# Second block: factors copied from PSUM, two products behind 1/rms, wide sums

## The chip, the cores and the metric

One Trainium2 chip, one of its eight cores. The metric is the time of one execution on the device in microseconds (us), here the median of three runs. The engines are named as in the profile: PE is TensorE's matmuls, PEld its weight loads, DVE is VectorE, ACT is ScalarE, POOL is GpSimd, SP issues DMAs.

## What is computed

Two transformer blocks run one after the other on x, 512 tokens by 1024 channels in float32. The change lies in the second block, whose two layers have this form:

```python
def second_block(x, ...):
    for i in range(DEPTH):                      # 2
        hn = rms_norm(x, norm_gains[i, 0])
        if kind == 0:
            m = stick_breaking_attention(hn, ...)
        elif kind == 1:
            m = dilated_attention(hn, ...)
        x = x + rms_norm(m, norm_gains[i, 1])
        f = conv_ffn(rms_norm(x, norm_gains[i, 2]), ...)
        x = x + rms_norm(f, norm_gains[i, 3])
    return x
```

with `rms_norm(x, g) = x * rsqrt(mean(x*x) + EPS) * g` over the 1024 channels of a token. So four times a matrix product m or f (the output projection of an attention, or the down projection of the feed-forward) is normalized, multiplied by a gain and added to x; after the first three of them the next layer's first projection follows.

## The kernel before

x lies in SBUF with channels on partitions: 8 chunks of 128 channels by 512 tokens. Every projection splits both operands into a high part (`hi`, float32r) and a low part (`lo`) and adds three matmuls per piece (`mm3`, L353 to L355). A weight tile of 128x1024 comes by DMA (`raw`), ScalarE casts it to `hi` (L294), and VectorE, or for every fourth one GpSimd, subtracts to get `lo` (L295); there are four buffers of each. A list `gates` can hold instructions: the next call of `split_w` takes its first entry, and its own instructions on the same engine are then issued after those.

The four places where m or f is normalized and added are held by the class `Mout`. The projection ahead of it (`gemm_4h` at place 1, `gemm_8h` at places 2 to 4) ends in `finish_h`, which treats the tokens in two halves of 256 (`hf` 0 and 1), each in four PSUM banks of two chunks. All eight PSUM banks are one pool of tiles of one bank each.

- `take(j, hf, ps)`: when bank j of a half is complete, ScalarE squares it (`PairSq.add`, L254), the squares are added over chunks (L259, L263; on GpSimd for half 1 unless it is the last place, else on VectorE), and VectorE writes bank times gain to `self.t` (L1963). At the last place, half 1, the gains wait until the sums are done, and j = 2, 3 go to ScalarE (L1961).
- `sums(hf)`: matmuls with a column of ones add the squares over partitions (L271), then `rstd_from` makes 1/rms: a square root on ScalarE (L192) and five small instructions on VectorE (L194 to L202).
- `spread(hf)`: two transposes (L177) put 1/rms as a row factor on all partitions, in a PSUM bank `self.rb`.
- `update(hf)`: for j = 0 to 3, `self.t` times the factor on VectorE (L1998), the addition to x (L1999, on GpSimd for j = 0 and 1, on VectorE for j = 2 and 3), and, unless it is the last place, the next projection's operand: high part on ScalarE (L2005), low part on VectorE (L2006). At the last place x is written out by DMA instead (L2001). `late()` squares the new x for the next norm (L254, L259, L263 on GpSimd).

For half 0 these steps lie inside the matmuls of half 1. For half 1 they lie inside the first block of the next projection (`halves_fm`): its matmuls for half 0 run first, channel by channel; after the fourth of eight come the sums, after the sixth the transposes, then the last two; then its matmuls for half 1, which need the new operand. The four weight tiles of that block are loaded and split ahead, by four calls of `m.pre(V)` in `finish_h`. At the last place nothing follows, and half 1's steps run alone.

Each engine works through its own queue in order. The framework's scheduler sets that order ahead of time, by program order among what it takes to be ready; `issue_after` adds an order.

Of the kernel before, what the change touches and what calls it, by code (L numbers as in the profile page):

```python
# [21 lines left out]
ALU = mybir.AluOpType  # L22
# [41 lines left out]
def build(tc, A, out, stop=None, dbg=None):  # L64
# [111 lines left out]
    def transpose(dst, src, idt=None):  # L176
        return PE.transpose(dst, src, ident if idt is None else idt)  # L177
# [38 lines left out]
    class SumSq:  # L216
# [6 lines left out]
        def add(self, ap):  # L223
            i = self.k % len(self.engs) if not self.last or self.k < NCH - 1 else len(self.engs)
            self.k += 1
            if i not in self.acc:
                self.acc[i] = t2()
                sq = S.activation(self.acc[i][:, : self.n], ap, AF.Square)
            else:
                q = t2()  # L230
                sq = S.activation(q[:, : self.n], ap, AF.Square)
                self.engs[i].tensor_tensor(self.acc[i][:, : self.n], self.acc[i][:, : self.n], q[:, : self.n], op=ALU.add)
            return sq
# [10 lines left out]
    class PairSq:  # L244
# [2 lines left out]
        def __init__(self, last=False):  # L247
            self.acc, self.k, self.last = ([], []), [0, 0], last

        def add(self, hf, ap, eng=G):  # L250
            acc = self.acc[hf]
            self.k[hf] += 1
            q = t2()
            ends = {"S": S.activation(q.rearrange("p (c t) -> p c t", c=2), ap, AF.Square)}  # L254
            a, b = q[:, 0:256], q[:, 256:512]
            if self.last and self.k[hf] == 4:
                acc += [a, b]
            elif not acc:
                ends[eng] = eng.tensor_tensor(a, a, b, op=ALU.add)  # L259
                acc.append(a)  # L260
            else:
                for v in (a, b):
                    ends[eng] = eng.tensor_tensor(acc[0], acc[0], v, op=ALU.add)  # L263
            return ends
# [1674 lines left out]
    class Mout:  # L1939
# [4 lines left out]
        def __init__(self, i, j, nxt, pre=nothing):  # L1944
            self.i, self.j, self.nxt, self.pre = i, j, nxt, pre
            self.t = [s8(), s8()]
            self.ss = PairSq(last=True)
            self.todo, self.ends = [], {}

        def pair(self, j, hf):  # L1950
            return self.t[hf][:, 512 * j : 512 * j + 512].rearrange("p (c t) -> p c t", c=2)

        def take(self, j, hf, ps):
            pv = ps.rearrange("p (c t) -> p c t", c=2)
            ends = self.ss.add(hf, pv, V if hf == 0 or self.nxt is None else G)
            g_ = vc("gains", 32 * self.i + 8 * self.j + 2 * j, 2)

            def gain():
                if last and j > 1:
                    for c in range(2):  # L1960
                        S.activation(self.pair(j, hf)[:, c], pv[:, c], AF.Copy, scale=g_[:, c : c + 1])  # L1961
                else:
                    V.tensor_tensor(self.pair(j, hf), pv, bc(g_[:, :, None], [128, 2, 256]), op=ALU.mult)  # L1963

            last = hf and self.nxt is None
            if not last:
                return gain()

            self.todo.append(gain)
            self.ends.update(ends)  # L1970

        def sums(self, hf):

            with contextlib.ExitStack() as st:
                for f in self.todo:
                    if f is self.todo[0]:
                        for e in self.ends.values():
                            st.enter_context(tc.issue_after(e.ins))
                    f()
            self.rs = self.ss.compact("sw", (hf,))  # L1980

        def spread(self, hf):

            self.rb = PS()
            for b in range(2):
                last = transpose(self.rb[:, b * 128 : b * 128 + 128], self.rs[:, b : b + 1].to_broadcast([128, 128]))
            return last

        def update(self, hf):

            ts = slice(256 * hf, 256 * hf + 256)
            if hf == 0 and self.nxt:
                self.h = Slabs(NCH)
                self.ss2 = PairSq()
            xp = lambda j: x[:, 2 * j : 2 * j + 2, ts]
            for j in range(4):
                mv, xs = self.pair(j, hf), xp(j)
                V.tensor_tensor(mv, mv, bc(self.rb[:, None, 0:256], [128, 2, 256]), op=ALU.mult)  # L1998
                (G if j in X_POOL else V).tensor_tensor(xs, xs, mv, op=ALU.add)  # L1999
                if self.nxt is None:  # L2000
                    nc.sync.dma_start(out[:, 2 * j : 2 * j + 2, ts], xs)  # L2001
                    continue
                for c in (2 * j, 2 * j + 1):
                    g_ = gains(*self.nxt, c)
                    S.activation(self.h.hi(c)[:, ts], x[:, c, ts], AF.Copy, scale=g_)  # L2005
                    V.scalar_tensor_tensor(self.h.lo(c)[:, ts], x[:, c, ts], g_, self.h.hi(c)[:, ts],  # L2006
                                           op0=ALU.mult, op1=ALU.subtract)

            def late():
                for j in range(4):  # L2010
                    if self.nxt:
                        self.ss2.add(hf, xp(j))

            return late
# [571 lines left out]
```

## Time and profile before

| | us |
|---|---|
| runs | 2198.81, 2201.05, 2202.95 |
| median | 2201.05 |
| profiled execution | 2198.05 |
| its span in the trace | 2196.2 |

| engine | busy us | share of the span |
|---|---|---|
| PE | 2081.6 | 95% |
| DVE | 1410.1 | 64% |
| ACT | 1113.0 | 51% |
| POOL | 507.5 | 23% |

The span runs from the first to the last instruction of the profiled execution; about 1.9 us lie around it. The four places are at about 1094 to 1163, 1494 to 1540, 1790 to 1837 and 2167 to 2196 us. Shares over the whole span say little about them: the waits and the order of the queues in those stretches have to be read.

### The profile page before, as it was taken

To read this page: it belongs to the slowest core of one execution; us is meant where nothing else is said; L and a number is where in the kernel's file an instruction comes from. 1 tells how busy PE (TensorE), PEld (TensorE's weight loads), DVE (VectorE), ACT (ScalarE), POOL (GpSimd) and SP (SyncE) were. 2 spreads that over 40 slices of the span, in tenths; PEclk is the share of its full clock that TensorE was granted. 3 is DMA by queue.
4 is the path that set the end of the run, shared out by engine and by line. 5 is a ranking of instruction groups with operands and counts; after the bars stand their busy time and mean duration, and the time that the engine had idled before them with its cause. 6 is when DMAs were issued, how large, how long until landed. Compare 5 with 4: busy or idle time off the path is not lost.

```text
span 2196.2 us, 32481 instructions
## 1 busy us (share of the span) xinstructions
PE 2081.6 (95%) x12321; PEld 1691.2 (77%) x12321; DVE 1410.1 (64%) x2298; ACT 1113.0 (51%) x1985; POOL 507.5 (23%) x510
## 2 busy tenths in 40 slices
PE   6889989999998998999999999999999989999997
PEld 1457767788866666766698888999778888888997
DVE  4678878677837987177757666526364578565633
ACT  3668854488836886244444333324243565333422
POOL 1010021488211314054431101014000023101011
PEclk9999999999999999999999999999999999999999
DMA  9789982123518995221112323322322212223321
GB/s 374 306 318 417 417 310 77 39 88 138 187 63 280 374 361 193 87 67 49 52 65 96 106 87 105 97 87 68 106 79 77 69 56 87 96 96 96 96 78 39
DMA packets 94096, 323.05 MB, mean 147 GB/s; under 512 B 11521, under 2 KB 17168, under 8 KB 93424
## 3 DMA queue, kind: packets, MB, share of 16 engines
q1 hardware_dynamic: 76480, 274.76, 34.9%
q0 software_dynamic: 7280, 25.83, 3.5%
q10 hardware_dynamic: 10176, 20.35, 2.5%
q8 instruction: 98, 1.61, 0.3%
q14 instruction: 62, 0.51, 0.1%
HBM read 300.63 MB, written 20.27 MB: 146 GB/s over the span
## 4 chain that ended last, share of the span: by engine, by line
PE 69%; DMA 11%; DVE 9%; POOL 4%; issue 3%; ACT 3%; SPq 0%; ACTq 0%; DVEq 0%; POOLq 0%
PE ps L353 19%; PE ps L355 19%; PE ps L354 18%; PE ps L177 4%; DMA s<-in_mgu_dram 2%; DMA raw<-in_mgu_dram 2%; DVE lo L295 1%; DMA raw<-in_wmod_dram 1%; PE ps L1786 1%; DMA s<-in_mdn_dram 1%; PE ps L380 1%; DMA raw<-in_mdn_dram 1%; PE ps L598 1%; POOL raw L1826 1%; ACT hi L294 1%
## 5 line engine op out<-in xcount | busy, mean ns | idle before, releaser
L353 PE MATMUL ps<-s,hi 128*128 128x512 f32 (+1 forms) x1440 | 513.0, 357 | 4.8 <-DVE s L1998 3.2
L354 PE MATMUL ps<-s,hi 128*128 128x512 f32 (+1 forms) x1440 | 504.8, 351 | 3.4 <-DVE s L2006 1.8
L355 PE MATMUL ps<-s,lo 128*128 128x512 f32 (+1 forms) x1440 | 507.0, 352 | 0.0
L294 ACT CAST hi<-raw 128x1024 fp32r<-128x1024 f32 x282 | 291.9, 1047 | 411.8 <-PE ps L354 335.2
L295 DVE TENSOR_TENSOR lo<-raw,hi 128x1024 fp32r<-128x1024 f32 x231 | 287.2, 1256 | 274.7 <-ACT hi L294 274.4
L295 POOL TENSOR_TENSOR lo<-raw,hi 128x1024 fp32r<-128x1024 f32 x51 | 122.9, 2410 | 870.6 <-ACT hi L294 870.6
L353 PEld LDWEIGHTS ps<-s,hi 128*128 128x128 f32 x1440 | 270.0, 188 | 46.4 <-issue 8.0
L354 PEld LDWEIGHTS ps<-s,hi 128*128 128x128 f32 x1440 | 270.5, 188 | 42.2 <-DVE s L2006 2.4
L355 PEld LDWEIGHTS ps<-s,lo 128*128 128x128 f32 x1440 | 270.3, 188 | 40.8 <-issue 0.5
L353 PE MATMUL ps<-hi,s 128*128 128x512 f32 (+1 forms) x528 | 216.4, 411 | 6.4 <-ACT hi L294 3.8
L354 PE MATMUL ps<-lo,s 128*128 128x512 f32 (+1 forms) x528 | 212.2, 402 | 2.5 <-DVE lo L295 2.5
L355 PE MATMUL ps<-hi,s 128*128 128x512 f32 (+1 forms) x528 | 211.4, 401 | 2.3 <-DVE s L1905 2.3
L354 PE MATMUL ps<-t2r,hi 128*128 128x256 f32 (+1 forms) x640 | 187.7, 293 | 0.0
L355 PE MATMUL ps<-t2r,lo 128*128 128x256 f32 (+1 forms) x640 | 187.3, 293 | 0.0
L353 PE MATMUL ps<-t2r,hi 128*128 128x256 f32 (+1 forms) x640 | 186.7, 292 | 0.0
L353 PEld LDWEIGHTS ps<-hi,s 128*128 128x128 f32 (+1 forms) x528 | 105.2, 199 | 32.4 <-ACT hi L294 6.5
L355 PEld LDWEIGHTS ps<-hi,s 128*128 128x128 f32 (+1 forms) x528 | 105.3, 199 | 28.8 <-DVE s L1905 3.9
L354 PEld LDWEIGHTS ps<-lo,s 128*128 128x128 f32 (+1 forms) x528 | 105.7, 200 | 25.4 <-DVE lo L295 2.9
L354 PEld LDWEIGHTS ps<-t2r,hi 128*128 128x128 f32 x640 | 120.5, 188 | 5.2 <-issue 2.5
L355 PEld LDWEIGHTS ps<-t2r,lo 128*128 128x128 f32 x640 | 120.4, 188 | 5.1 <-issue 2.5
L353 PEld LDWEIGHTS ps<-t2r,hi 128*128 128x128 f32 x640 | 120.7, 189 | 2.7
L295 DVE TENSOR_TENSOR lo<-s,hi 128x1024 fp32r<-128x1024 f32 x97 | 113.9, 1218 | 8.2 <-ACT hi L294 6.6
(391 smaller groups left out, 3704.7 us busy)
## 6 DMA issues: line engine op xcount, KB each, us to landing
raw<-in_up_dram SPq DMA_DIRECT2D x88, 512.0 KB
s<-in_mgu_dram SPq DMA_DIRECT2D x64, 512.0 KB
raw<-in_mgu_dram SPq DMA_DIRECT2D x44, 512.0 KB
raw<-in_down_dram SPq DMA_DIRECT2D x44, 512.0 KB
raw<-in_dilqkv_dram SPq DMA_DIRECT2D x36, 512.0 KB
s<-in_mdn_dram SPq DMA_DIRECT2D x34, 512.0 KB
raw<-in_wmodT_dram SPq DMA_DIRECT2D x32, 512.0 KB
s<-in_wmod_dram SPq DMA_DIRECT2D x30, 512.0 KB
```

The source lines that it names most:

```text
L177: return PE.transpose(dst, src, ident if idt is None else idt)
L294: S.copy(hi, raw)
L295: eng.tensor_tensor(lo, raw, hi, op=ALU.subtract)
L353: mm(ps, ahi, bhi, start=start, stop=False)
L354: mm(ps, ahi, blo, start=False, stop=False)
L355: return mm(ps, alo, bhi, start=False, stop=stop)
L380: mm(ps[32 * kk : 32 * kk + 32, :], cs[:, 4 * u + kk, :], raw[kk // 2][:, kk % 2 * 512 : kk % 2 * 512 + 512], start=(u == 0), stop=(u == 1 ...
L598: mm(q.psl[32 * k : 32 * k + 32, : q.n], w, v, start=q.seen == 0, stop=q.seen == 3, tile_position=(0, 32 * k))
L1786: mm(po_[c][o : o + 64, qb * 128 : qb * 128 + 128], vview[:, kc, c // 2 * 64 : c // 2 * 64 + 64], PTs[h_][:, kc * 128 : kc * 128 + 128], s ...
L1826: G.tensor_tensor(w, w, crow, op=ALU.mult)
```

## The change

`PairSq.add` gets a form `wide`, used for half 1 of the last place only: the squares of two chunks stay side by side in one tile of 128x512, later pairs are added to it in one instruction, and both columns of chunks go on to the matmul with ones. `take` puts the gain products of j = 2 and 3 of half 1 into a list `behind` (places 1 to 3). `sums` issues them after the last instruction of 1/rms and puts that instruction into `gates` for the next `split_w`. `spread` copies the row factors to an SBUF tile on ScalarE. `update` reads the PSUM bank for j = 0 and the copy for j = 1 to 3.

```diff
--- before.py
+++ after.py
@@ -247,7 +247,7 @@
         def __init__(self, last=False):
             self.acc, self.k, self.last = ([], []), [0, 0], last
 
-        def add(self, hf, ap, eng=G):
+        def add(self, hf, ap, eng=G, wide=False):
             acc = self.acc[hf]
             self.k[hf] += 1
             q = t2()
@@ -255,6 +255,12 @@
             a, b = q[:, 0:256], q[:, 256:512]
             if self.last and self.k[hf] == 4:
                 acc += [a, b]
+            elif wide:
+                if not acc:
+                    acc += [a, b]
+                    self.sum = q
+                else:
+                    ends[eng] = eng.tensor_tensor(self.sum, self.sum, q, op=ALU.add)
             elif not acc:
                 ends[eng] = eng.tensor_tensor(a, a, b, op=ALU.add)
                 acc.append(a)
@@ -1945,14 +1951,14 @@
             self.i, self.j, self.nxt, self.pre = i, j, nxt, pre
             self.t = [s8(), s8()]
             self.ss = PairSq(last=True)
-            self.todo, self.ends = [], {}
+            self.todo, self.ends, self.behind = [], {}, []
 
         def pair(self, j, hf):
             return self.t[hf][:, 512 * j : 512 * j + 512].rearrange("p (c t) -> p c t", c=2)
 
         def take(self, j, hf, ps):
             pv = ps.rearrange("p (c t) -> p c t", c=2)
-            ends = self.ss.add(hf, pv, V if hf == 0 or self.nxt is None else G)
+            ends = self.ss.add(hf, pv, V if hf == 0 or self.nxt is None else G, hf and self.nxt is None)
             g_ = vc("gains", 32 * self.i + 8 * self.j + 2 * j, 2)
 
             def gain():
@@ -1963,6 +1969,8 @@
                     V.tensor_tensor(self.pair(j, hf), pv, bc(g_[:, :, None], [128, 2, 256]), op=ALU.mult)
 
             last = hf and self.nxt is None
+            if hf and self.nxt and j > 1:
+                return self.behind.append(gain)
             if not last:
                 return gain()
 
@@ -1978,13 +1986,19 @@
                             st.enter_context(tc.issue_after(e.ins))
                     f()
             self.rs = self.ss.compact("sw", (hf,))
+            if self.behind:
+                gates.append((rends[1],))
+                with tc.issue_after(rends[1].ins):
+                    while self.behind:
+                        self.behind.pop(0)()
 
         def spread(self, hf):
 
             self.rb = PS()
             for b in range(2):
-                last = transpose(self.rb[:, b * 128 : b * 128 + 128], self.rs[:, b : b + 1].to_broadcast([128, 128]))
-            return last
+                transpose(self.rb[:, b * 128 : b * 128 + 128], self.rs[:, b : b + 1].to_broadcast([128, 128]))
+            self.rbs = t2()[:, 0:256]
+            S.copy(self.rbs, self.rb[:, 0:256])
 
         def update(self, hf):
 
@@ -1995,7 +2009,8 @@
             xp = lambda j: x[:, 2 * j : 2 * j + 2, ts]
             for j in range(4):
                 mv, xs = self.pair(j, hf), xp(j)
-                V.tensor_tensor(mv, mv, bc(self.rb[:, None, 0:256], [128, 2, 256]), op=ALU.mult)
+                rb = self.rb[:, 0:256] if j == 0 else self.rbs
+                V.tensor_tensor(mv, mv, bc(rb[:, None, :], [128, 2, 256]), op=ALU.mult)
                 (G if j in X_POOL else V).tensor_tensor(xs, xs, mv, op=ALU.add)
                 if self.nxt is None:
                     nc.sync.dma_start(out[:, 2 * j : 2 * j + 2, ts], xs)
```

## Rows read from the trace of the kernel before

**Rows 1.** Page, part 4: the chain that ended last, by engine.

```profile
PE 69%; DMA 11%; DVE 9%; POOL 4%; issue 3%; ACT 3%; SPq 0%; ACTq 0%; DVEq 0%; POOLq 0%
```

**Rows 2.** PE's waits in 1505 to 1530 (place 2), then 1126 to 1152 (place 1).

```profile
engine line waited for: us in total, times, longest us
PE ps L177 <- DVE sm L202: 1.6, 1, 1.6
PE ps L353 <- DVE s L1998: 1.5, 1, 1.5
PE ps L354 <- DVE s L2006: 0.6, 1, 0.6
...
PE ps L353 <- ACT s L2005: 0.7, 1, 0.7
...
PE ps L177 <- DVE sm L202: 0.5, 1, 0.5
```

**Rows 3.** Timeline of DVE at place 2: start, duration; xN merges neighbours.

```profile
1504.10 0.69 DVE L1998 TENSOR_TENSOR s<-s,ps 128x512 f32<-128x512 f32 x1 [1.66 <-PE ps L177]
1504.70 1.22 DVE L295 TENSOR_TENSOR lo<-raw,hi 128x1024 fp32r<-128x1024 f32 x1
1505.84 0.68 DVE L1998 TENSOR_TENSOR s<-s,ps 128x512 f32<-128x512 f32 x1
1507.66 1.38 DVE L2006 SCALAR_TENSOR_TENSOR s<-x,vec,s 128x256 fp32r<-128x256 f32 x2 [1.14 <-ACT s L2005]
...
1518.07 1.27 DVE L1963 TENSOR_TENSOR s<-ps,vec 128x512 f32<-128x512 f32 x2
1519.27 1.38 DVE L295 TENSOR_TENSOR lo<-raw,hi 128x1024 fp32r<-128x1024 f32 x1
...
1522.08 0.16 DVE L202 SCALAR_TENSOR_TENSOR sm<-sm,sm 128x2 f32<-128x2 f32 x1
1522.83 1.88 DVE L1998 TENSOR_TENSOR s<-s,ps 128x512 f32<-128x512 f32 x3 [0.59 <-PE ps L177]
...
1532.95 1.85 DVE L2006 SCALAR_TENSOR_TENSOR s<-x,vec,s 128x256 fp32r<-128x256 f32 x2
```

**Rows 4.** Timelines of ACT and POOL at the start of place 2's first update.

```profile
1503.33 1.05 ACT L294 CAST hi<-raw 128x1024 fp32r<-128x1024 f32 x1 [1.74 <-issue]
1507.12 0.91 ACT L2005 ACTIVATE s<-x,vec 128x256 fp32r<-128x256 f32 x2 [2.73 <-POOL x L1999]
...
1504.86 3.49 POOL L1999 TENSOR_TENSOR x<-x,s 128x512 f32<-128x512 f32 x2 [27.94 <-DVE s L1998]
```

**Rows 5.** Lines over the whole span: ns min/median/max, first and last start; waits.

```profile
L1998 DVE TENSOR_TENSOR s<-s,ps x32: 671/679/689, 1129.4 to 2189.2; 128x512 f32<-128x512 f32 x32
L1999 POOL TENSOR_TENSOR x<-x,s x16: 1259/1306/2224, 1130.2 to 2189.4; 128x512 f32<-128x512 f32 x16
L1999 DVE TENSOR_TENSOR x<-x,s x16: 676/764/1481, 1135.6 to 2191.1; 128x512 f32<-128x512 f32 x16
L1641 ACT COPY s<-ps x6: 372/373/374, 364.0 to 384.0; 128x256 f32<-128x256 f32 x6
its engine sat idle before it (us, times) until:
  DVE t L1615: 7.8, 6
```

**Rows 6.** Timelines of DVE and of PE at place 4, from half 0's update on.

```profile
2177.00 2.48 DVE L1998 TENSOR_TENSOR s<-s,ps 128x512 f32<-128x512 f32 x4 [1.92 <-PE ps L177]
2179.39 2.08 DVE L1999 TENSOR_TENSOR x<-x,s 128x512 f32<-128x512 f32 x2
2181.92 1.87 DVE L263 TENSOR_TENSOR t<-t,t 128x256 f32<-128x256 f32 x4
2187.40 2.48 DVE L1998 TENSOR_TENSOR s<-s,ps 128x512 f32<-128x512 f32 x4 [0.84 <-PE ps L177]
2189.80 2.00 DVE L1999 TENSOR_TENSOR x<-x,s 128x512 f32<-128x512 f32 x2
...
2183.94 1.47 PE L271 MATMUL ps<-ones,t 128*128 128x1 f32 x12 [1.53 <-DVE t L263]
```

## The prediction

> **What bounds the kernel now.** The chain that ended last comes first: TensorE holds 69% of it [rows 1], so what matters is where TensorE stands still. The change touches only the four places of the second block where one matrix product is normalized and added to x before the next can start: after the first attention (from about 1104 us), after the first feed-forward (1494), after the second attention (1790) and at the end (2167). I call them places 1 to 4. The list of TensorE's waits comes second [rows 2]. At place 2 it waits three times: 1.5 us for the PSUM bank of the row factors, which the last of four products (L1998) gives back, 1.6 us for 1/rms of half 1 (L202), 0.6 us for the first low part of half 1 (L2006). Place 3 repeats that to within 0.2 us. Place 1 has no bank wait, 0.5 us for 1/rms and 0.7 for the first high part (L2005) of half 1. Third, the timelines of VectorE, ScalarE and GpSimd at place 2 [rows 3, 4]: VectorE is hardly idle from 1504.1 on, and its order is what the reader should follow. Fourth, place 4 [rows 6], where TensorE has nothing left and every step is on the path.
>
> So TensorE's 3.7 us of waits at place 2 are one debt paid in three parts. All end at the same queue: VectorE with GpSimd beside it, update of half 0, then 1/rms, then update of half 1. Removing an early wait only makes TensorE arrive earlier at the next. I therefore cost the change on VectorE's queue.
>
> **Part by part. The copy.** Each of eight spreads gets a ScalarE copy of 128x256 from PSUM. The kernel has one of that form elsewhere: 0.37 us (L1641) [rows 5]. The same rows show what its first reader pays: that copy waited six of six times (7.8 us) for a VectorE instruction that read other columns of the same bank. Two readers of one bank go one after the other. In the new code the copy is written ahead of the first product, so product 0 (still from PSUM) waits for it: 0.37 plus 0.04 hand-over, 0.4 us. At place 2, half 0, ScalarE is also in a weight cast until 1504.38 [rows 4], so the copy ends at 1504.75 and the product starts at 1504.8 in place of 1504.10: 0.7. Bounds: 0.4 if the copy goes ahead of the cast, 0 if product 0 goes first. I take 0.7 there, and 0.4 where ScalarE is idle (place 4).
>
> **Products 1 to 3 from SBUF.** Product forms that read PSUM took 671 to 689 ns in all 32 cases, whatever GpSimd did. Additions on VectorE with both inputs in SBUF and the same size took 676 to 1481 ns, and the same additions on GpSimd 1259 to 2224 [rows 5]. So with both inputs in SBUF, VectorE and GpSimd exclude each other, and with one in PSUM they don't. The change moves 24 products from the free kind into the excluding kind, each just where GpSimd adds chunks 0 and 1 to x. Two L2006 back to back show how turns are taken: 1.38 us for the pair that met one GpSimd instruction, 1.85 for a pair that met two [rows 3]; GpSimd gets in between.
> [...]
> Nothing is gained per product: 676 ns is the fastest with SBUF alone, 679 the median with PSUM [rows 5].
> [...]
> The price at place 2, half 0 [rows 3, 4]: GpSimd's first addition is held by the weight split until 1505.92 and done when ScalarE starts at 1507.12, so 1.2 us. Product 1, which ran at 1505.84 beside it, must now wait until 1507.1 and ends at 1507.7 in place of 1506.52. That pushes GpSimd's second addition by 0.7, and the L2006 pair behind it, which lost 0.5 to it anyway, ends 0.7 later. Product 3 meets GpSimd's sums of squares: 0.6 more. Together 1.3. Bounds: 0 (VectorE always first) and 2 x 1.2 = 2.4.
>
> **Two norm-weight products behind 1/rms.** At places 1 to 3, two L1963 leave the queue ahead of 1/rms: 1518.07 to 1519.27, so 1.2 us earlier [rows 3]. They aren't gone: they stand right behind L202, ahead of half 1's first product, which came 0.6 us after L202 ended (1522.24 to 1522.83). Two L1963 take 1.27, so that product comes 0.7 later relative to 1/rms; the 0.4 of the copy hides under them. Who waits: product 0, GpSimd's addition, ScalarE's L2005, L2006, TensorE. Then GpSimd's addition of chunk 0 is held by product 1: 0.6.
>
> **The ordered split.** The order is put on the next split made after the sums of half 1. The four splits of the next weight block were made earlier (among them the one at 1519.27), so the ordered one is the first of the block after, and its weight buffer is given back only by TensorE's work on half 1. That lies behind 1/rms already: nothing is won or lost, and the split at 1519.27 stays ahead of 1/rms.
>
> **Place 2 summed.** 1/rms: +0.7 (copy) +1.3 (products) -1.2 (moved) = +0.8. First low part of half 1: +0.8 +0.7 +0.6 = +2.1. TensorE, without its bank wait (the bank is free after product 0), is at the transposes 1.5 us sooner and waits there for 1/rms; the early 1.5 us buys nothing. It resumes half 1 2.1 us later than 1526.5. Place 3 has the same order and waits: +2.1. Place 1 has the same update with no bank wait, and I take +2.1 too. Behind each place TensorE runs on without slack, so all 6.3 us reach the end.
>
> **Place 4** [rows 6]. Half 0's update took 4.5 us (2177.00 to 2181.47). Now: copy 0.4, then products and additions of 0.6 with two GpSimd additions of 1.2 in between: 0.6 + 0.6 + 1.2 + 0.6 + 1.2 + 0.6 + 0.6 + 0.7 = 6.1. VectorE is free 2.0 later, at 2183.5. The sums of squares in wide form: one instruction less at the start and two of 0.6 to 0.7 for four, 1.3 in place of 2.3: done at 2184.8 against 2183.8, +1.0. The sum of squares now has 8 columns, not 6, so 16 matmuls for 12 at 1.47/12 = 0.12 each: +0.5. Half 1's update, the very end: 4.4 us (2187.40 to 2191.80) becomes 0.4 + 6.1: +2.1. Place 4: +3.6. Bound below: if nothing excludes, half 0 gives -1.0 + 0.4 + 0.5 and half 1 +0.4: +0.3.
>
> **How the numbers follow.** 3 x 2.1 + 3.6 = +9.9 us. The profiled execution took 2198.05 us (span 2196.2), so 2208.0 by its own time; the runs shown have a median of 2201.05 (2198.81 to 2202.95), so I predict 2201.05 + 9.9 = 2211.0 us. Within 0.2% (4.4 us) no measurement of this kernel can tell a change.
>
> **Rivals.**
> 1. *The products don't pay* (chance 0.23): VectorE's products keep 0.68 us because GpSimd is left waiting instead, and its additions have slack. Then places 1 to 3 give 0.7 - 1.2 + 0.7 = +0.2 each and place 4 +0.3: 2202, no change that can be told. For it: a lone wait of GpSimd costs TensorE nothing. Against it: the first addition of each update starts ScalarE and so TensorE.
> 2. *The order wins* (0.10), the other side: the split at 1519.27 lands behind 1/rms, so 1/rms comes a further 1.3 us sooner (two such splits, 2.6, at place 1), and the products don't pay. Places 2 and 3: 0.2 - 1.3 = -1.1 each; place 1: -2.4; place 4: +0.3; in all -4.3, 2196.7. It decides from the point where L202 ends before TensorE reaches the transposes. Against it: that split was made before the order is set, and it feeds the matmuls right after the transposes.
> 3. *Banks* (0.10), further up: the delayed products hold two PSUM banks of half 1 until after 1/rms. With four for the next block, two more for sums and factors fill all eight; if the sum of squares must wait for one, about 1 us more at each of three places: 2214.
> Forecast: 0.57, of which 0.05 costs under half of its sum and falls within 0.2%. Slower 0.52 + 0.10 = 0.62, same 0.23 + 0.05 = 0.28, faster 0.10. The range takes in the forecast, rivals 1 and 3 and the spread of the runs: 2199.5 to 2214.0.
>
> **What would show it.** Right: L1998 splits in two kinds, eight near 0.68 us and 24 reaching well above 1 us beside GpSimd; TensorE's wait for L1998 is gone while its waits for L202 and L2006 at places 2 and 3 grow to more than 3.7 us; the chain's end has about 6 us between half 1's first product and the last addition. Wrong: SBUF products of 0.68 us throughout, first products that start without waiting for the copy, or L202 well over 1 us sooner after the transposes of half 0 with the first L2006 of half 1 sooner as well.

## The result, and the profile after

The changed kernel takes 2216.74 us (median of 6 runs, 2212.81 to 2217.73) against 2200.63 us (6 runs, 2198.81 to 2204.68) before: a ratio of 1.0067, 95% interval 1.0056 to 1.0078. It is slower, as forecast, but by 16 us where 9.9 were predicted. Its profiled execution took 2217.73 us, span 2216.0 (before 2196.2). Each kernel numbers its own lines: L271, L295, L354, L1963, L1998 and L2006 of the kernel before are L277, L301, L360, L1969, L2013 and L2021 in the changed one, whose L2001 is the copy.

The chain that ended last has moved from TensorE towards VectorE, a little (compare [rows 1]):

```profile
PE 68%; DVE 11%; DMA 10%; issue 5%; POOL 3%; ACT 3%; ACTq 0%; SPq 0%; POOLq 0%; DVEq 0%
```

**The four places measured.** I take a place from the first square of half 0 (ScalarE, L254) to the square root of the next norm (L192 on four columns), the last place to the end of the span. In the changed kernel place 2 lies between these rows of ScalarE's timeline:

```profile
1500.02 1.28 ACT L254 ACTIVATE t<-ps 128x512 f32<-128x512 f32 x2 [7.91 <-PE ps L361]
...
1548.25 0.26 ACT L192 ACTIVATE sm<-ps,epst 128x4 f32<-128x4 f32 x1 [0.56 <-PE ps L277]
```

Windows cut at such times give one row for each place: its length, the busy time of TensorE's matmuls (with their count), of its weight loads, VectorE, ScalarE and GpSimd, then the granted clock, share of the DMA engines and GB/s. First the kernel before:

```profile
1104.46:1160.15 55.69, 53.88 (x454) 53.17 (x453) 36.04 (x59) 26.28 (x45) 26.77 (x24) 1.00 0.21 67
1494.14:1536.65 42.51, 38.88 (x325) 37.99 (x324) 34.72 (x57) 24.28 (x43) 26.25 (x24) 1.00 0.19 63
1790.69:1832.83 42.14, 38.20 (x322) 37.40 (x321) 34.69 (x57) 24.27 (x42) 26.17 (x24) 1.00 0.19 63
2167.52:2196.23 28.71, 17.01 (x142) 16.31 (x140) 17.71 (x38) 8.05 (x15) 5.05 (x4) 0.83 0.21 74
```

and the changed one:

```profile
1108.65:1166.68 58.03, 54.23 (x454) 53.24 (x453) 41.40 (x59) 27.14 (x46) 26.50 (x24) 1.00 0.22 64
1500.02:1548.25 48.23, 41.87 (x325) 40.93 (x324) 39.76 (x57) 25.35 (x44) 27.72 (x24) 0.93 0.19 56
1801.44:1849.79 48.35, 42.02 (x322) 40.95 (x321) 40.49 (x57) 25.24 (x45) 27.29 (x24) 0.93 0.19 55
2184.17:2215.99 31.82, 18.27 (x146) 17.52 (x144) 19.82 (x35) 8.79 (x17) 6.70 (x4) 0.79 0.19 66
```

The places grew by 2.3, 5.7, 6.2 and 3.1 us, 17.4 in all; predicted were 2.1, 2.1, 2.1 and 3.6. (The rest of the span's difference, +4.2 us ahead of place 1 and -1.8 between places, lies where nothing was changed.) Length less busy matmuls is TensorE's idle time: 1.8, 3.6, 3.9 and 11.7 us before, 3.8, 6.4, 6.3 and 13.6 after. That is +9.0 us of waiting, close to the forecast's 9.9. The other 8.4 us are not waits: **the same 325 matmuls of place 2 took 3.0 us longer**, the 322 of place 3 3.8 us longer, at a mean granted clock of 0.93 in place of 1.00. (The remaining 1.6 us lie at place 4, with four matmuls more and a lower clock, and at place 1.)

TensorE's waits at place 2 after, for [rows 2] before, and at place 3 the same to 0.1 us:

```profile
PE ps L277 <- DVE s L1969: 3.1, 1, 3.1
PE ps L360 <- DVE s L2021: 2.4, 2, 1.4
PE ps L359 <- ACT s L2020: 0.8, 1, 0.8
```

The 1.5 us for the row factors' bank and the 1.6 for 1/rms are gone. In their place half 1's sum of squares (L277) waits 3.1 us for a PSUM bank, given back by a gain product (L1969). Once the matmuls have resumed, the granted clock falls to 0.50 in this finer cut of place 2, and 15 matmuls fit into 3 us where 28 did:

```profile
1512.00:1515.00 3.00, 3.00 (x28) 3.00 (x26) 3.00 (x4) 1.96 (x3) 2.81 (x2) 1.00 0.63 175
1521.00:1524.00 3.00, 1.38 (x12) 1.17 (x10) 3.00 (x5) 3.00 (x7) 2.22 (x3) 1.00 0.30 55
1527.00:1530.00 3.00, 3.00 (x15) 3.00 (x16) 2.77 (x8) 0.26 (x1) 2.77 (x4) 0.50 0.55 145
```

VectorE's timeline, for [rows 3], says why the bank is late:

```profile
1510.29 1.22 DVE L301 TENSOR_TENSOR lo<-raw,hi 128x1024 fp32r<-128x1024 f32 x1 [2.15 <-ACT hi L300]
1511.43 0.68 DVE L2013 TENSOR_TENSOR s<-s,ps 128x512 f32<-128x512 f32 x1
1512.03 4.10 DVE L2013 TENSOR_TENSOR s<-s,t 128x512 f32<-128x512 f32 x3
1516.05 2.15 DVE L2021 SCALAR_TENSOR_TENSOR s<-x,vec,s 128x256 fp32r<-128x256 f32 x4
1518.12 2.37 DVE L2014 TENSOR_TENSOR x<-x,s 128x512 f32<-128x512 f32 x2
1520.42 1.76 DVE L301 TENSOR_TENSOR lo<-raw,hi 128x1024 fp32r<-128x1024 f32 x1
1522.10 2.61 DVE L2021 SCALAR_TENSOR_TENSOR s<-x,vec,s 128x256 fp32r<-128x256 f32 x4
1524.64 1.27 DVE L1969 TENSOR_TENSOR s<-ps,vec 128x512 f32<-128x512 f32 x2
```

In the kernel before, these rows of VectorE stand between those of [rows 3]:

```profile
1512.68 1.85 DVE L2006 SCALAR_TENSOR_TENSOR s<-x,vec,s 128x256 fp32r<-128x256 f32 x2
...
1515.60 1.27 DVE L1963 TENSOR_TENSOR s<-ps,vec 128x512 f32<-128x512 f32 x2
1516.80 1.34 DVE L2006 SCALAR_TENSOR_TENSOR s<-x,vec,s 128x256 fp32r<-128x256 f32 x2
```

The order itself has changed. Before: product, split, product, two low parts; and two of half 0's eight low parts were still to come when the first two gains of half 1 ran. Now the split stands ahead of the first product, the four products follow in one row, and the first gains come after all eight low parts. Counted from the first square of the place, the first gain begins at 21.5 us before and at 24.6 now. The likely reason, which no run shows directly: with the copy in front, the first product isn't ready when the scheduler reaches it, so it takes the split first, and everything behind shifts.

The products (L2013) and GpSimd's additions (L2014), ns min/median/max, for [rows 5]:

```profile
L2013 DVE TENSOR_TENSOR s<-s,t x24: 681/1748/1798, 1135.6 to 2209.2; 128x512 f32<-128x512 f32 x24
L2013 DVE TENSOR_TENSOR s<-s,ps x8: 677/682/689, 1135.0 to 2206.3; 128x512 f32<-128x512 f32 x8
...
L2014 POOL TENSOR_TENSOR x<-x,s x16: 1642/1700/1750, 1135.8 to 2208.7; 128x512 f32<-128x512 f32 x16
```

Place 4, VectorE and then TensorE, for [rows 6]:

```profile
2194.04 0.69 DVE L2013 TENSOR_TENSOR s<-s,ps 128x512 f32<-128x512 f32 x1 [2.33 <-ACT t L2001]
2194.65 4.10 DVE L2013 TENSOR_TENSOR s<-s,t 128x512 f32<-128x512 f32 x3
2198.67 1.28 DVE L2014 TENSOR_TENSOR x<-x,s 128x512 f32<-128x512 f32 x2
2199.88 1.48 DVE L263 TENSOR_TENSOR t<-t,t 128x512 f32<-128x512 f32 x2
...
2206.33 0.69 DVE L2013 TENSOR_TENSOR s<-s,ps 128x512 f32<-128x512 f32 x1 [1.25 <-ACT t L2001]
...
2210.88 1.28 DVE L2014 TENSOR_TENSOR x<-x,s 128x512 f32<-128x512 f32 x2
...
2201.41 2.53 PE L277 MATMUL ps<-ones,t 128*128 128x1 f32 x16 [2.16 <-DVE t L263]
```

### The profile page after: what moved, and what is told of

The parts are those of the page before. It is cut to its first block, busy times and chain, and to the rows that moved or that the text cites. A ratio compares the mean times of both kernels' runs of the same rounds, so it can differ in the third digit from the quotient of the medians.

```text
span 2216.0 us, 32498 instructions
## 1 busy us (share of the span) xinstructions
PE 2091.7 (94%) x12325; PEld 1700.6 (77%) x12325; DVE 1427.8 (64%) x2295; ACT 1116.8 (50%) x1993; POOL 516.0 (23%) x510
## 4 chain that ended last, share of the span: by engine, by line
PE 68%; DVE 11%; DMA 10%; issue 5%; POOL 3%; ACT 3%; ACTq 0%; SPq 0%; POOLq 0%; DVEq 0%
PE ps L359 18%; PE ps L361 18%; PE ps L360 18%; PE ps L177 4%; DMA s<-in_mgu_dram 2%; DVE lo L301 2%; DMA raw<-in_mgu_dram 1%; DMA raw<-in_wmod_dram 1%; DMA s<-in_mdn_dram 1%; DVE s L2013 1%; PE ps L1792 1%; PE ps L386 1%; DMA raw<-in_mdn_dram 1%; PE ps L604 1%; POOL raw L1832 1%
## 5 line engine op out<-in xcount | busy, mean ns | idle before, releaser
L360 PE MATMUL ps<-s,hi 128*128 128x512 f32 (+1 forms) x1440 | 510.0, 354 | 8.7 <-DVE s L2021 7.4
L301 DVE TENSOR_TENSOR lo<-raw,hi 128x1024 fp32r<-128x1024 f32 x231 | 286.8, 1254 | 281.3 <-ACT hi L300 280.9
L301 POOL TENSOR_TENSOR lo<-raw,hi 128x1024 fp32r<-128x1024 f32 x51 | 123.2, 2416 | 870.4 <-ACT hi L300 870.4
L360 PEld LDWEIGHTS ps<-s,hi 128*128 128x128 f32 x1440 | 273.9, 190 | 48.9 <-DVE s L2021 9.1
L359 PEld LDWEIGHTS ps<-s,hi 128*128 128x128 f32 x1440 | 273.1, 190 | 45.2 <-issue 4.4
L360 PE MATMUL ps<-lo,s 128*128 128x512 f32 (+1 forms) x528 | 212.4, 402 | 2.8 <-DVE lo L301 2.8
L360 PE MATMUL ps<-t2r,hi 128*128 128x256 f32 (+1 forms) x640 | 187.1, 292 | 0.0
L360 PEld LDWEIGHTS ps<-lo,s 128*128 128x128 f32 (+1 forms) x528 | 105.7, 200 | 25.9 <-DVE lo L301 3.3
L360 PEld LDWEIGHTS ps<-t2r,hi 128*128 128x128 f32 x640 | 120.7, 189 | 5.2 <-issue 2.5
L301 DVE TENSOR_TENSOR lo<-s,hi 128x1024 fp32r<-128x1024 f32 x97 | 113.9, 1218 | 8.3 <-ACT hi L300 8.0
```

What stands on the lines that cost most here:

```text
L301: eng.tensor_tensor(lo, raw, hi, op=ALU.subtract)
L359: mm(ps, ahi, bhi, start=start, stop=False)
L360: mm(ps, ahi, blo, start=False, stop=False)
```

## The experiments

The kernels do the same up to place 1, yet place 1 began anywhere from 1104.5 to 1118.9 us in their profiled executions. So for single parts the place lengths are the finer measure. But each is from one execution: where two kernels have the same code at a place, lengths agree to 0.4 us if the clocks do, and differ by up to 1.5 us if they don't. The table has, for each kernel and place, length / TensorE's idle time / mean granted clock, each from one window row as above.

| kernel | place 1 | place 2 | place 3 | place 4 | sum of lengths |
|---|---|---|---|---|---|
| before | 55.7 / 1.8 / 1.00 | 42.5 / 3.6 / 1.00 | 42.1 / 3.9 / 1.00 | 28.7 / 11.7 / 0.83 | 169.0 |
| after | 58.0 / 3.8 / 1.00 | 48.2 / 6.4 / 0.93 | 48.4 / 6.3 / 0.93 | 31.8 / 13.6 / 0.79 | 186.4 |
| copy_only | 61.5 / 4.4 / 0.94 | 49.6 / 6.5 / 0.90 | 48.3 / 6.2 / 0.93 | 32.6 / 14.8 / 0.79 | 192.0 |
| copy_unread | 57.2 / 2.1 / 0.97 | 45.8 / 4.0 / 0.93 | 45.5 / 3.9 / 0.92 | 29.5 / 12.3 / 0.83 | 178.0 |
| behind_only | 56.5 / 2.8 / 1.00 | 42.2 / 3.2 / 1.00 | 41.8 / 3.4 / 1.00 | 29.2 / 11.5 / 0.79 | 169.6 |
| wide_only | 55.6 / 1.8 / 1.00 | 42.1 / 3.6 / 1.00 | 42.1 / 3.6 / 1.00 | 28.8 / 11.0 / 0.80 | 168.7 |
| no_copy | 56.5 / 2.8 / 1.00 | 42.2 / 3.4 / 1.00 | 41.8 / 3.1 / 1.00 | 28.7 / 11.0 / 0.83 | 169.1 |
| after_copyfirst | 58.3 / 2.5 / 0.97 | 50.6 / 7.5 / 0.90 | 50.5 / 7.2 / 0.90 | 32.9 / 13.8 / 0.76 | 192.3 |
| unread_copyfirst | 57.9 / 2.6 / 0.97 | 45.5 / 4.9 / 0.96 | 45.2 / 4.9 / 0.96 | 29.5 / 12.3 / 0.81 | 178.0 |
| after_gainsfirst | 59.1 / 3.6 / 0.97 | 45.6 / 6.5 / 1.00 | 47.1 / 5.1 / 0.93 | 31.7 / 13.5 / 0.79 | 183.5 |
| unread_gainsfirst | 57.2 / 1.8 / 0.97 | 43.4 / 3.0 / 0.96 | 42.7 / 2.8 / 0.96 | 30.1 / 12.5 / 0.79 | 173.4 |
| before_dveadds | 56.2 / 1.1 / 0.97 | 43.3 / 2.8 / 0.96 | 43.0 / 2.7 / 0.96 | 29.8 / 12.0 / 0.79 | 172.3 |
| after_dveadds | 56.0 / 2.0 / 1.00 | 44.8 / 4.2 / 0.96 | 46.0 / 4.0 / 0.93 | 29.2 / 11.5 / 0.81 | 176.0 |
| unread_fill | 55.6 / 2.1 / 1.00 | 43.8 / 2.3 / 1.00 | 43.3 / 2.1 / 1.00 | 30.4 / 12.5 / 0.78 | 173.1 |
| after_fill | 58.0 / 3.9 / 1.00 | 48.3 / 3.8 / 0.93 | 46.3 / 3.6 / 0.96 | 32.4 / 13.7 / 0.77 | 185.0 |
| gains_on_act | 55.2 / 1.5 / 1.00 | 44.6 / 4.4 / 0.96 | 44.0 / 4.6 / 0.96 | 28.7 / 11.7 / 0.84 | 172.5 |

**The parts, one at a time.** The copy alone, read by products 1 to 3 (copy_only), on the kernel before:

```diff
+            self.rbs = t2()[:, 0:256]
+            S.copy(self.rbs, self.rb[:, 0:256])
...
+                rb = self.rb[:, 0:256] if j == 0 else self.rbs
+                V.tensor_tensor(mv, mv, bc(rb[:, None, :], [128, 2, 256]), op=ALU.mult)
```

> The copy of the row factors and products 1 to 3 from it, and nothing else of the change. Theory A (VectorE and GpSimd exclude each other once a product has both inputs in SBUF, and the longer queue of VectorE gives the bank for the sum of squares back late): most of the loss is here, +11 to +14 us, places 2 and 3 at 47 to 48 us in place of 42.5 and 42.1, with TensorE waiting about 3 us for a norm-weight product's bank. Theory B (the delayed norm-weight products hold the banks): only the exclusion is left, +2 us at each of four places, +8 to +9, and no such bank wait.

The same copy with no reader, the products all from PSUM (copy_unread: the last two lines left out):

> The copy is made, but all four products read PSUM as before, so only the copy itself and the wait for it are left. Theory A: products stay at 0.68 us, the loss is 8 waits of 0.4 us and a little queueing behind casts and splits, +2 to +4 us. Theory C (the wait for the copy and the order that it brings are what costs): nearly all of the +16 us.

The two gains and the split behind 1/rms alone (behind_only), and the wide additions alone (wide_only), each the change's own lines on the kernel before:

> Only the two norm-weight products and the split ordered behind 1/rms; factors stay in PSUM, sums of squares as before. Theory A: 1/rms of half 1 comes about 1 us sooner, the first product of half 1 about as much later, -1 to +1 us. Theory B: the held banks cost 3 us at places 2 and 3, +5 to +7 us.

> Only the wide sums of squares at place 4: one VectorE instruction less at the start, two of 0.68 us in place of four of 0.43, and 16 matmuls for 12. Every theory: -0.3 us at place 4 (28.7 to 28.4 us), which the median can't show.

And the change without its copy (no_copy):

> The changed kernel without its copy: all products read PSUM, the two delayed gain products and the split stay behind 1/rms, the last half's squares stay added two chunks at a time; nothing is left out. Theory A (all the loss comes in with the copy, by its order and by the SBUF operands; the other two edits are worth nothing either way): places at 56.4, 42.2, 41.8 and 28.8 us as with the edits one by one, together within 1 us of before, ratio 0.998 to 1.001. Theory B (the delayed gains cost by the PSUM banks that they hold, whatever the copy does): the sum of squares waits for a bank at places 2 and 3 here too, and the places are 1 us longer each or more, ratio 1.001 or more.

Measured, as ratios to the kernel before: copy_only 1.0087 [1.0056, 1.0118], copy_unread 1.0036 [1.0016, 1.0056], behind_only 0.9993 [0.9970, 1.0015], wide_only 0.9990 [0.9966, 1.0015], no_copy 1.0011 [0.9991, 1.0032]. So the whole loss comes in with the copy; the other two edits together leave the places at 169.1 us against 169.0. Copy_only lost some 19 us, more than either theory gave it, and copy_unread some 8, between its two.

Copy_unread is the surprise. Nothing reads the copy, and the rows of its places 2 and 3

```profile
1497.42:1543.24 45.82, 41.79 (x325) 40.95 (x324) 36.07 (x57) 25.14 (x44) 24.92 (x24) 0.93 0.18 58
1797.68:1843.19 45.51, 41.58 (x322) 40.88 (x321) 36.10 (x57) 25.14 (x44) 24.94 (x24) 0.92 0.18 58
```

show idle times (4.0 and 3.9 us) hardly above before (3.6 and 3.9), but matmuls 2.9 and 3.4 us slower. At place 2 the two waits of 1.5 and 1.6 us [rows 2] have merged into one:

```profile
PE ps L271 <- DVE s L1963: 3.0, 1, 3.0
PE ps L353 <- ACT s L2006: 0.6, 1, 0.6
PE ps L354 <- DVE s L2007: 0.4, 1, 0.4
```

VectorE's gains there, and in unread_gainsfirst (below), which moves them ahead again:

```profile
1520.39 2.47 DVE L1963 TENSOR_TENSOR s<-ps,vec 128x512 f32<-128x512 f32 x4
...
1522.73 2.47 DVE L1967 TENSOR_TENSOR s<-ps,vec 128x512 f32<-128x512 f32 x4
```

From the first square of the place to the first gain it is 23.0 us here and 21.3 in unread_gainsfirst (21.5 before). So the bank comes back 1.5 us later than before, which is only half of the 3.0. The rest is an old wait moved: TensorE no longer waits 1.5 us for the row factors' bank and reaches the sum of squares that much sooner, at 20.8 us, where before it was there at 22.3, just after the bank was free.

Copy_only less copy_unread is the price of the SBUF operand: 2.3, 2.5, 2.3 and 2.5 us more idle time at the four places, and 2.1, 1.3, 0.5 and 0.6 us of slower matmuls.

**Which order does it?** Two kernels put the cast of the split behind the copy on ScalarE, so that the first product gets ahead of the split again (after_copyfirst on the changed kernel, unread_copyfirst on copy_unread; `m.cp` is the copy):

```diff
-        m.pre(V)
+        with tc.issue_after(m.cp.ins):
+            m.pre(V)
```

> The changed kernel, with the cast of the split on ScalarE (second half of the 1/rms step) issued behind the PSUM-to-SBUF copy; nothing is left out. Theory A (the order at the head of VectorE's queue costs): the subtraction of the split no longer stands ahead of the first product, which starts about 1.2 us earlier after the transposes, the low parts follow earlier, and TensorE's wait for the first low part (1.4 us) falls below 0.5 us: each of the first three places 1 us shorter or more, together -3 us or more. Theory B (the four SBUF products in a row and the late gains cost, the head doesn't): the first product starts earlier, the bank wait of the sum of squares stays at about 3 us, and the places stay within 0.5 us of 58.0, 48.2 and 48.4 us.

> The kernel before with the copy made but not read (all products from PSUM), and with the cast of the split on ScalarE issued behind the copy, so that the first product stands ahead of the split on VectorE again. The output is the same; nothing is left out. The copy unread alone gave places of 57.2, 45.8, 45.5 and 29.5 us against 55.7, 42.5, 42.1 and 28.7 us before, with the sum of squares waiting 3.0 us for a PSUM bank at places 2 and 3. Theory A (the late gains of half 1 carry the 3.3 us, by the bank): they are still last in VectorE's order, so the wait stays near 3 us and places 2 and 3 stay at 45 to 46 us. Theory B (the split ahead of the first product carries it): the places fall back to within 1 us of before, 42 to 43.5 us. A copy that costs only its own wait (0.4 to 0.7 us) would also give about 43 us.

Measured 1.0090 [1.0070, 1.0111] and 1.0043 [1.0028, 1.0059]: no gain, and on the changed kernel places 2 and 3 grew by 2.4 and 2.1 us. The first product did go first, but the gains stayed last, and the sum of squares waited 5.3 us for its bank at place 2 with the former, 2.7 with the latter. Mending the head of the queue alone doesn't help.

Two kernels put the low parts of chunks 6 and 7 behind the first gains instead (after_gainsfirst, unread_gainsfirst; `m.gained` is the second gain product, `low` issues one low part):

```diff
+                    if hf == 0 and j > 2:
+                        self.lows.append(low)
+                    else:
+                        low()
...
+            with tc.issue_after(m.gained.ins):
+                for f in m.lows:
+                    f()
```

> The changed kernel, with the low parts of chunks 6 and 7 of half 0 issued on VectorE behind the first two gain products of half 1; nothing else is moved, and nothing is left out. Theory A (the queue's order sets when the PSUM bank comes back): in the changed kernel the first gain product of half 1 stands behind the low parts of half 0, and the matmul of the sum of squares waits about 3.1 us for the bank that it gives back, at the second and third place. Two low parts ahead of it fewer are 2 x 0.6 us, so the bank comes back 1.2 us earlier or more, the wait falls from 3.1 us to 1.9 us or less, and the two places fall from 48.2 and 48.4 us to some 46 to 47 us; about 2.5 to 5 us of the whole, so 0.997 to 0.999 of the changed kernel. Theory B (the SBUF operands alone set the place, the bank wait lies beside it): the wait shrinks, but TensorE then waits for the delayed low parts in its third product instead, and both places stay at 48 to 49 us.

> The kernel before with the copy made but not read, and with the low parts of chunks 6 and 7 of half 0 issued on VectorE behind the first two gain products of half 1; nothing is left out. All products read PSUM, so that no product is slowed by the additions on GpSimd; what is left of the change is the copy and the order that comes with it. The copy unread alone had places 2 and 3 at 45.8 and 45.5 us (before 42.5 and 42.1), the sum of squares waiting 3.0 us for a PSUM bank. Theory A (the late gains carry that by the bank): the wait falls to 1 us or less and both places return to 42.7 to 44 us; with place 1 at 56 to 57.5 us and place 4 at 29.5 us as with the copy unread, the whole falls by 3 to 5 us against it, to 2205 to 2208 us (ratio 1.001 to 1.002). Theory B (the split ahead of the first product carries it): the wait goes elsewhere (the third product's low parts come later) and both places stay at 45 to 46 us.

Measured 1.0054 [1.0034, 1.0073] and 1.0017 [0.9995, 1.0038]. Unread_gainsfirst has all four gains ahead of those low parts; its bank wait fell from 3.0 to 1.3 us and places 2 and 3 from 45.8 and 45.5 to 43.4 and 42.7: the late gains carry most of it. Even so the clock fell there, behind the 1.3 us wait, to a mean of 0.59 over this stretch:

```profile
1525.00:1528.00 3.00, 3.00 (x18) 3.00 (x18) 3.00 (x4) 0.26 (x1) 2.76 (x4) 0.59 0.00 0
```

In after_gainsfirst the sum of squares waits 2.0 and 1.8 us, now for GpSimd's squares. It has one order at places 2 and 3 but not one clock: 1.00 and 45.6 us at place 2, 0.93 and 47.1 at place 3.

**Is it the operand, or GpSimd?** All additions to x on VectorE, in the kernel before and in the changed one:

```diff
-X_POOL = (0, 1)
+X_POOL = ()
```

> The kernel before with all additions to the stream on VectorE and none on GpSimd; nothing is left out. It is the other half of the pair with the changed kernel so moved. Products stay at 0.67 to 0.69 us under every theory; four more additions of 0.68 us per half on VectorE make each place up to 2 to 3 us longer than before if VectorE sets it, and leave it within 0.5 us of before if GpSimd's additions of 1.3 to 2.2 us had been as late.

> The changed kernel with all additions to the stream on VectorE and none on GpSimd; nothing is left out. Theory A (the SBUF operand costs only while a GpSimd addition runs beside the product): every product takes 0.67 to 0.69 us, none 1.2 to 1.8 us. At place 4 four slow products of two halves no longer cost, but four more additions of 0.68 us come onto VectorE; measured against the kernel before with the same move, place 4 differs by the copy's 0.8 us less the wide additions' gain, within -0.5 and +1.0 us instead of +3.1 us. Theory B (a product of two SBUF operands is slower by itself, or slowed by any other engine's reads): products j = 2 and 3 stay at 1.2 us or more, and place 4 stays 2 to 3 us above the kernel before with the same move.

Measured 1.0013 [0.9993, 1.0033] and 1.0032 [1.0010, 1.0053]. With no addition on GpSimd the products from SBUF (after_dveadds) are as fast as those from PSUM at the median, 685 ns against 684, and only the slowest reach 1.2 us:

```profile
L2013 DVE TENSOR_TENSOR s<-s,t x24: 683/685/1229, 1137.5 to 2204.6; 128x512 f32<-128x512 f32 x24
L2013 DVE TENSOR_TENSOR s<-s,ps x8: 677/684/689, 1136.9 to 2201.6; 128x512 f32<-128x512 f32 x8
```

and the change costs 3.7 us over the four places, not 17.4 (the ratios' intervals overlap); at place 4 nothing is left of it. What is left at places 2 and 3 (+1.5 and +3.0) stands beside a bank wait of 3.4 us at place 2, where before_dveadds has 0.9.

**Bank or clock?** If the bank's late return delayed the chain by itself, hiding the wait would change nothing. So 22 matmuls of zeros were put on TensorE into that wait, at places 2 and 3 (unread_fill, after_fill); `zr` is a column of zeros, and they add nothing to the bank they accumulate in:

```diff
+                if hf == 0 and i == S_AT and (m.i, m.j) != (0, 1):
+                    for _ in range(22):
+                        last = mm(banks[3][:, ts], zr.to_broadcast([128, 128]), rhs(part[0])[0][:, ts], start=False, stop=False)
```

> The kernel before with the copy made but not read, and 22 matmuls of zeros (128x256, about 0.12 us each, added to a bank that TensorE is filling anyway) issued on TensorE right ahead of half 1's sum of squares at places 2 and 3; nothing is left out. The order of VectorE's queue is that of the copy unread, so the PSUM bank comes back as late as there. With the copy unread, TensorE had 325 and 322 matmuls at places 2 and 3 in 41.8 and 41.6 us at a mean granted clock of 0.93 and 0.92 (before: 38.9 and 38.2 us at 1.00) and stood idle 4.0 and 3.9 us (before 3.6 and 3.9). Theory A (one wait of 3.0 us lets the granted clock fall, and the slow matmuls behind it are the loss): the filler takes 2.6 us of that wait, the clock stays at 0.99 to 1.00, the matmuls of the kernel take 38.5 to 39.5 us again, idle falls to some 1.4 us, and both places return to 42 to 43.5 us, the whole about 5 to 6 us shorter than with the copy unread. Theory B (the bank's late return delays everything behind it by itself): the filler only hides the wait, and places 2 and 3 stay at 45 to 46 us.

> The changed kernel with the same 22 matmuls of zeros on TensorE right ahead of half 1's sum of squares at places 2 and 3; nothing is left out. In the changed kernel places 2 and 3 are 48.2 and 48.4 us at a granted clock of 0.93, with 41.9 and 42.0 us of matmuls and 6.4 and 6.3 us of idle TensorE. Theory A (the clock): the clock stays at 0.99 to 1.00 and both places fall by 2.5 to 3.5 us, to 45 to 46 us; what remains over the kernel before, about 2.5 us each, is the waits for VectorE's slower products. Theory B: both places stay at 48 to 49 us.

Unread_fill (1.0037 [1.0015, 1.0059]) at places 2 and 3:

```profile
1496.88:1540.63 43.75, 41.48 (x347) 40.47 (x346) 36.12 (x57) 25.13 (x45) 25.25 (x24) 1.00 0.18 61
1794.82:1838.14 43.32, 41.24 (x344) 40.38 (x343) 36.13 (x57) 25.15 (x45) 25.22 (x24) 1.00 0.19 62
```

Twenty-two matmuls more, and both places 2.1 and 2.2 us shorter than with the copy unread: the clock stays at 1.00, and less about 22 x 0.12 us the kernel's own matmuls take 38.8 and 38.6 us again (before 38.9 and 38.2). In these executions, then, the lower clock was the loss. The runs do not show it in time: 1.0037 against copy_unread's 1.0036, where 5 to 6 us less were expected. They show part of it in the clock: its mean over a run lies 0.0022 below that of the kernel before, and 0.0040 below with the copy unread. Nor does the wait alone set the clock: at place 1, which has no filler, unread_fill has the same waits as copy_unread (1.5 and 0.6 us), but a clock of 1.00 in place of 0.97, and 55.6 us in place of 57.2.

After_fill (1.0086 [1.0054, 1.0118], no better than the changed kernel's 1.0067) split the cases. At place 3 the clock held behind the filled wait (first row) and fell only later, behind the waits for half 1's slowed products (second row), and the place is 2.1 us shorter than in the changed kernel. At place 2 it fell behind the filled wait too, though only 0.6 us were left of it (third row), and the place stayed at 48.3:

```profile
1826.00:1829.00 3.00, 3.00 (x27) 3.00 (x28) 2.82 (x7) 0.26 (x1) 2.76 (x4) 1.00 0.24 74
...
1835.00:1838.00 3.00, 2.90 (x18) 2.90 (x19) 3.00 (x7) 2.88 (x7) 1.62 (x2) 0.74 0.02 5
...
1525.00:1528.00 3.00, 3.00 (x19) 3.00 (x19) 2.82 (x7) 0.26 (x1) 2.76 (x4) 0.64 0.25 83
```

**A way to gain?** VectorE's queue ahead of 1/rms is what all waits end at, so two gains were given to ScalarE (gains_on_act):

```diff
-                if last and j > 1:
+                if hf and j > 1:
```

> The kernel before, with the gain products of the last two pairs of chunks of half 1 done on ScalarE at all places (four instructions of 128x256 in place of two of 128x512 on VectorE), as the kernel before does at the last place; nothing is left out. Theory A (VectorE's queue ahead of 1/rms of half 1 sets the step): 2 x 0.63 us leave VectorE's queue ahead of 1/rms, ScalarE has room there, and each of places 1 to 3 falls by 0.5 to 1.2 us: -1.5 to -3.5 us, ratio 0.9985 to 0.9993. Theory B (ScalarE's queue takes the place: its squares of the next pair and the cast wait behind the gains): 0 to +3 us.

Measured 1.0014 [1.0005, 1.0024]: no gain. Place 1 is 0.5 us shorter, places 2 and 3 2.0 and 1.9 us longer: TensorE now waits for ScalarE's high part of half 1,

```profile
PE ps L353 <- ACT s L2005: 2.4, 1, 2.4
```

and the clock fell to a mean of 0.96. None of the kernels in the table is measurably faster than the kernel before.

## Why the prediction was off

**The direction was right, and so was the cause given for the products.** The copy with products from SBUF costs more than the edits behind 1/rms give back. The products came in two kinds, as forecast, but with 16 of the 24 slowed, not all: the first from SBUF in each half, which begins 0.2 us ahead of GpSimd's addition, keeps 0.68 us. At place 2 that addition follows VectorE's row at 1512.03:

```profile
1512.19 3.38 POOL L2014 TENSOR_TENSOR x<-x,s 128x512 f32<-128x512 f32 x2 [28.91 <-DVE s L2013]
```

The SBUF operand costs beside GpSimd's additions: the pair with the additions moved shows it, with a median product from SBUF of 1748 ns before the move and 685 after. The trace of the changed kernel shows the two engines finishing by turns. At place 2 the first addition ends at 1513.88 us, the second product at 1514.43, the second addition at 1515.57 and the third product at 1516.13: a product some 0.55 us after an addition, an addition 1.14 us after a product, where the kernel before took 0.68 for a product and 1.30 for an addition [rows 5]. Half 1's third product from SBUF, at places 1 to 3, took 1.22 us beside an addition of squares on GpSimd. Nothing was gained per product, as forecast: 685 ns from SBUF with the additions moved, 684 from PSUM in the same kernel.

**Place 4** was predicted at +3.6 and took +3.1. Its terms for VectorE held: the first product waits 0.4 us longer for the copy (2.33 and 1.25 us after, 1.92 and 0.84 in [rows 6]); half 0's products and additions take 5.9 us (2194.04 to 2199.95) where 4.5 became, without the copy, 6.1; two wide additions take 1.5 where 1.3 was estimated. The matmuls' term was 0.6 us too small: sixteen matmuls with ones took 2.53 us and not 1.96, the last of them at a clock of 0.50 (2202.7 to 2204.0 us). The tail was forecast 0.9 us too long: 0.3 of it in half 1's products and additions (5.8, not 6.1), the rest because from the last addition to the end it is 3.8 us now and was 4.4 before, which the sum had left out.

**The step that failed** is the pricing of waits at places 2 and 3: "TensorE's 3.7 us of waits at place 2 are one debt paid in three parts", and "all 6.3 us reach the end" one for one. As a debt it was near: idle time at places 1 to 3 grew by 2.0, 2.7 and 2.4 us against 2.1 each. But it was paid elsewhere. The prediction's own sign, waits for 1/rms and the first low part of more than 3.7 us together, did not come: TensorE waits 3.1 us for the bank of the sum of squares, none for 1/rms, 2.4 for low parts. And the matmuls behind that wait ran at 0.50, as did some at place 2 behind the waits for half 1's products (1537 to 1540 us): 3.0 and 3.8 us at places 2 and 3 that no term of the sum held. The sum took the time of the matmuls as fixed; before the change no place but the last (0.83) showed a granted clock below 1.00, with no wait above 1.7 us at places 2 and 3. In the changed kernel the clock was 0.50 behind a wait of 3.1 us at both; before_dveadds, at 0.96 at place 2 with no wait there above 0.9 us, shows that a single long wait isn't needed.

**The second miss** lies one step earlier: the copy was costed at its own wait (0.7), with VectorE's order as it was. The copy changed the order, and that is where the single long wait comes from. Rival 3 named the right wait, a bank for the sum of squares, with the wrong cause: the two delayed products. It stands in copy_unread, where nothing is delayed, and is absent at both places in behind_only; the products that come late there are the first two gains, behind half 0's low parts.

**Place 1** came out at +2.3 against +2.1, +2.0 of it idle time. That no matmul time came on top was in part luck: copy_only had +5.9 there with the clock at 0.94, the changed kernel +2.3 at 1.00.

**The products' term** was somewhat small: 1.9 us (1.3 and 0.6) at place 2 against 2.5 of idle time. The copy's was too large: 0.7 us against 0.4 of idle time in copy_unread.

**The two L1963 behind 1/rms** were to give 0.5 us a place net. Alone they took 0.4 and 0.5 us from the idle time at places 2 and 3, as said, and added 1.0 at place 1, where TensorE waited 1.8 us for 1/rms (0.5 before [rows 2]); why, the runs don't show. **The wide form** alone changed place 4 by 0.1 us.

Left open: what exactly makes the clock fall. At places 2 and 3 it fell in every kernel with a wait of 2.3 us or more, and stayed at 1.00 in before, behind_only, no_copy and unread_fill, whose listed waits are 1.7 us or less, and in wide_only. But it also fell with a longest wait of 1.8 us (after_gainsfirst, place 3), 1.3 (unread_gainsfirst, after_fill) and 0.9 (before_dveadds), and it stood at 1.00 at place 2 of after_gainsfirst with a wait of 2.0 and 6.5 us of idle time. The rows show that the clock carries the matmuls' extra time, not what sets it off each time. That hiding the wait makes the whole run shorter is not shown.

## What to carry to other kernels

When an edit puts an instruction ahead of a queue that a scheduler orders, read the new order before costing anything: a copy that nobody read made the four places 9 us longer. Price a TensorE wait twice, as idle time and by the granted clock of the stretch behind it. Here three waits of 3.7 us in all left the clock at 1.00, and one of 3.0 us with two short ones, 4.0 in all, did not. An operand moved from PSUM to SBUF was free only where GpSimd was not adding at that moment: 0.68 us a product against 1.75.

## What the runs showed of the hardware

- VectorE and GpSimd, both with two SBUF inputs of 128x512: the product goes from 0.68 to 1.75 us, the addition from 1.30 to 1.70 [rows 5], so both slow down; the three products in a row at place 4 took 4.10 us.
- VectorE's read of a PSUM bank began only after ScalarE's copy of 128x256 out of it had ended, 0.4 us later than without the copy. Whether the chip or the framework makes it wait, the runs don't show.
- TensorE's granted clock fell to 0.50 behind a single wait of 3.0 to 3.1 us in the middle of dense matmuls, in the changed kernel at places 2 and 3 and in copy_unread at place 2. Twenty-two matmuls of zeros in that wait kept it at 1.00 behind the wait in three of four cases; in the fourth, place 2 of after_fill, the mean over the 3 us behind it was 0.64.
